# Second norm of a hybrid decoder layer: tile 4 joins the tiles that go through DRAM, rows dealt by stepped reads, two tiles scaled and evicted by ScalarE, the last tile's transposes inside a product

## The chip, the cores and the metric

The kernel runs on one core of a Trainium2 chip. The metric is the device time of one execution in microseconds (us); before the change it is 947.92 us, the median of three runs (947.66 to 949.35).

Names in the profile: PE is TensorE's matmuls, PEld its weight loads, DVE is VectorE, ACT is ScalarE, POOL is GpSimd, SP is SyncE, which issues most of the DMAs. L99 is line 99 of the kernel before. `b<-c,b` says that a buffer of the ring `b` is written from `c` and `b`.

## The reference, cut to what matters

```python
for l in range(DEPTH):                                # DEPTH = 1, 1024 tokens and 16 meta tokens
    u = rmsnorm(h, g_pre_mix[l]); z = u @ w_in[l]     # q, k, v, x_rec, y_rec
    ...                                               # attention and gated recurrence
    mix = jnp.concatenate([attn, rec], axis=-1) @ w_out[l]
    h = h + rmsnorm(mix, g_post_mix[l])
    u = rmsnorm(h, g_pre_ffn[l])                      # the second norm
    f = jnp.square(jax.nn.relu(u @ w_ff1[l])) @ w_ff2[l]
    h = h + rmsnorm(f, g_post_ffn[l])
```

Width is 1024, the feed-forward width 4096, all in float32. Each float32 product is made of three fp32r matmuls (high x high, high x low, low x high: lines 125, 130, 131), so every operand is split into a high part (a cast on ACT, L96) and a low part (a difference on DVE, L99).

## The kernel before, in words

The 1024 tokens are eight tiles of 128 rows. For each tile `out_mm` multiplies the mixed heads by `w_out` into two PSUM banks. `out_norm` takes the sum of squares (ACT, L1052), a power on POOL (L176), scales and adds the residual on DVE (L1058, L1061), stores `h` (SP, L1062) and takes the squares of `h` for the second norm (ACT, L1064, and POOL again). `out_scale` multiplies `h` by the second norm's factor.

What follows needs the second norm's result `u` transposed: features on partitions, tokens along the free axis. There are two ways to it.

- Tiles 0 to 3 (`u2_store`, L1010 to L1018): one DVE operation multiplies `h` by the factor and by `g_pre_ffn` and deals the 1024 columns into four groups, column by column. A DVE transpose of 32x32 blocks follows, a store to DRAM (`u2_dram`) by SP, and four reads back (`u2_read`, L1022), which wait for the store. The result lies in `u2f[0]`, four buffers [128, 16, 2, 32]: 16 groups of 32 tokens, two feature blocks each.
- Tiles 4 to 7 (`out_scale` L1071 and `u2_tiles`, L1083 to L1094): DVE scales, PE transposes eight blocks of 128x128 against the identity into two banks of the tag `o`, and the banks are evicted with `g_pre_ffn` as a column factor: the first four blocks by ACT in four operations of 128 columns (L1094), the last four by DVE in two of 256 (L1088); for tile 6 ACT takes all eight. The result lies in `u2f[1]`, four buffers [128, 2, 512].

The first feed-forward product is one step of a Strassen-like scheme on halves of features and tokens. `u2f[0]` holds the first four tiles and `u2f[1]` the last four, with two buffers for each half of the features. `t_sums` (L1236) makes differences and sums of the four quarters in pieces of tokens, as tiles come in: `t3 = u2f[1][2+i] - u2f[1][i]`, `t2 = t3 + u2f[0][i]`, and the split `ot2` of `t2`. `p1(p)` is the product with the first quarter, `p2(p)` that with the second, evicted by a DVE addition (L1234). `prep_a(p)` loads two blocks of `w_ff1`, makes their sums and differences on DVE (L1109) and splits them (L96, L99). The main loop over 16 blocks then multiplies `ot2` and `ot3` (the split of `t3`).

The order on each engine comes from a scheduler that goes by the order of the code and by a timeline of its own; `behind(name, ins)` pins one instruction behind another on the same engine. Buffers come from rings (`raw` 2, `ws` 5, `a` 16, `b` 17, `c` 8, `d` 4, `e` 2), so a buffer's reuse is a wait too.

Of the kernel before, what the change touches and what calls it, by code (L numbers as in the profile page):

```python
# [9 lines left out]
F32 = mybir.dt.float32  # L10
F32R = mybir.dt.float32r
AF = mybir.ActivationFunctionType
# [25 lines left out]
def hybrid_layer(  # L38
# [961 lines left out]

    u2f = [[slot("c", [P, 16, 2, 32]) for _ in range(4)], [None] * 4]
    u2_dram = dpool.tile([4, 4, P, 2 * P], F32, name="u2_dram")
    gpre_b = slot("ws", [P, D])
    nc.scalar.dma_start(gpre_b, g_pre_ffn[0].partition_broadcast(P))

    def dealt(t_):
        return t_.rearrange("p (k d b) -> p k d b", k=KC, b=4)

    def u2_store(t, h, rs, tmp):
        ins = nc.vector.scalar_tensor_tensor(  # L1010
            tmp.rearrange("p (b k d) -> p k d b", b=4, k=KC), dealt(h), rs,
            dealt(gpre_b), op0=ALU.mult, op1=ALU.mult,
        ).ins
        if t < 3:
            behind(summed[t + 1], ins)
        y = slot("e", [P, D])
        nc.vector.transpose(y, tmp)
        nc.sync.dma_start(u2_dram[t].rearrange("a (d b) r -> (a d) (b r)", b=4), y)  # L1018

    def u2_read(t):  # L1020
        for q in range(4):
            nc.sync.dma_start(  # L1022
                u2f[0][q][:, 4 * t : 4 * t + 4].rearrange("p a k t -> p a (k t)"),
                u2_dram[t, :, :, 64 * q : 64 * q + 64].rearrange("a p r -> p a r"),
            )
# [19 lines left out]
    def out_norm(t, po):  # L1045
# [17 lines left out]
        ssq2 = small.tile([P, 1], F32, name="ssq", tag="ssq")  # L1063
        nc.scalar.activation(xr, h, AF.Square, scale=RMS_SC, accum_out=ssq2)  # L1064
        return h, xr, rstd_of([ssq2])

    def out_scale(t, h, xr, rs2):
        if t < 4:
            u2_store(t, h, rs2, xr)
            return None  # L1070
        nc.vector.tensor_scalar(xr, h, rs2, None, op0=ALU.mult)  # L1071
        return xr

    def u2_tiles(t, xn):
        half = t // 4
        if u2f[half][0] is None:
            u2f[half] = [slot("c", [P, 2, 512]) for _ in range(4)]
        o = (t % 4) * P
        for k4 in range(0, KC, 4):
            pt = bank("o", (P, 4, P))  # L1080
            for i in range(4):
                kc = k4 + i
                nc.tensor.transpose(pt[:, i, :], xn[:, kc * P : (kc + 1) * P], ident)  # L1083
            for i in range(0, 4, 2):
                kc = k4 + i
                dst = u2f[half][kc // 2]
                if k4 and t != 6:
                    nc.vector.tensor_tensor(  # L1088
                        dst[:, :, o : o + P], pt[:, i : i + 2, :],
                        g_ffn_col[:, kc : kc + 2].to_broadcast([P, 2, P]), op=ALU.mult,  # L1090
                    )
                    continue
                for n in range(2):
                    nc.scalar.activation(  # L1094
                        dst[:, n, o : o + P], pt[:, i + n, :], AF.Copy,
                        scale=g_ffn_col[:, kc + n : kc + n + 1],
                    )

    w1v = w_ff1.rearrange("(b k p) c -> b p k c", b=2, p=P)

    def w1_load(dst, b, p, a0, a1):
        c0 = 256 * p
        nc.sync.dma_start(dst, w1v[b][:, :, c0 + P * a0 : c0 + P * a1])

    def combine(dst, x0, x1, op):
        return nc.vector.tensor_tensor(dst, x0, x1, op=op).ins  # L1109

    def rows(t_, c=slice(0, 512)):
        if len(t_.shape) == 4:
            return t_[:, c.start // 32 : c.stop // 32]
        return t_[:, :, c].rearrange("p k (g t) -> p g k t", t=32)

    def operand(tiles):
        pairs = []
        for t_ in tiles:
            hi, lo = pair("b", [P, 2, 512])
            if len(t_.shape) == 4:  # L1120
                split(rows(hi), rows(lo), t_)
            else:
                split(hi, lo, t_)
            pairs.append((hi, lo))
        return pairs

    def product(acc, w, op, first, after=None):
        wh, wl = w
        for kc in range(4):
            hh, ll = op[kc // 2]  # L1130
            mm3(
                acc, (wh[:, kc, :], wl[:, kc, :]), (hh[:, kc % 2, :], ll[:, kc % 2, :]),
                first and kc == 0, kc == 3, after if kc == 0 else None,
            )
# [5 lines left out]
    def prep_a(p, late=None):  # L1140
        r0 = slot("raw", [P, 4, 256])
        w1_load(r0, 0, p, 0, 2)
        r1 = slot("a" if 2 <= p < 14 else "d", [P, 4, 256])
# [22 lines left out]
    def early(b, p0, hl, tag="raw"):  # L1166
        raw = slot(tag, [P, 2, 4, P])
        for k in range(2):
            w1_load(raw[:, k], b, p0 + k, 0, 1)
        split(*hl, raw)  # L1170
        return {p0 + k: (hl[0][:, k], hl[1][:, k]) for k in range(2)}

    a11_early, a12_early = {}, {}

# [61 lines left out]
    def t_sums(c):  # L1236
        for i in range(2):
            combine(t3[i][:, :, c], u2f[1][2 + i][:, :, c], u2f[1][i][:, :, c], ALU.subtract)
            combine(rows(t2[i], c), rows(t3[i], c), rows(u2f[0][i], c), ALU.add)
            hi, lo = ot2[i]  # L1240
            split(hi[:, :, c], lo[:, :, c], t2[i][:, :, c])

    for t in range(8):
        po = pos[t] if t < 4 else out_banks(t)
        out_mm(t, po, range(6 if t < 4 else 0, KC))
        if t > 5:
            u2_tiles(t - 2, xns[t - 2])
        if t == 7:
            t3 = [slot("a", [P, 2, 512]) for _ in range(2)]
            t2 = [slot("a", [P, 2, 512]) for _ in range(2)]  # L1250
# [4 lines left out]
        if 1 <= t <= 4:  # L1255
            u2_read(t - 1)
        if t == 7:
            t_sums(slice(0, 2 * P))
            u2_tiles(6, xns[6])
# [24 lines left out]
    for i in range(2):  # L1284
        behind(urgent, split(*ot3[i], t3[i]))
    token_low = mark[0]
# [3 lines left out]
    def t_rest(k):  # L1290
        i = k % 2
        if k < 2:
            behind(mark[0], combine(rows(u2f[1][i]), rows(u2f[1][i]), u2f[0][i], ALU.subtract))
        elif k < 4:
            behind(mark[0], combine(rows(t2[i]), u2f[0][2 + i], rows(t2[i]), ALU.subtract))
        else:
            hl = pair("a", [P, 2, 512])
            late = mark[0]
            behind(late, split(*hl, t2[i]))
            for n in range(2):  # L1300
                nc.gpsimd.dma_start(t4_dram[:, n, 2 * i : 2 * i + 2, :], f32(hl[n]))
# [339 lines left out]
```

## Time and profile before

| what | before |
|---|---|
| median of three runs | 947.92 us (947.66 to 949.35) |
| the profiled execution | 947.43 us, of it 945.7 in the span of the profile |
| granted TensorE clock | 0.998 |
| PE, weight loads, DVE, ACT, POOL busy | 99%, 83%, 70%, 53%, 14% of the span |
| DVE busy from 290 to 340 us of the span | 42.34 of 50 us |
| chain that ended last | 97% PE |

The profile is one execution. A row of the timeline gives start, duration, engine, line and shapes, and in brackets the engine's idle time before it and what ended that. A group row gives the count, the sum and the mean of the durations, and the idle time before them. Matmuls are pipelined: one lasts 0.39 us, but the next starts 0.23 us after it, so distances are taken from start to start.

### The profile page before, as it was taken

The numbers are of one execution on the slowest core, as the hardware profiler recorded it, in microseconds if no ns is written. First come the engines' busy times: TensorE is split into PE (matmuls) and PEld (weight loads), VectorE is DVE, ScalarE is ACT, GpSimd is POOL, SyncE is SP. The second block draws the span as 40 slices with busy tenths as digits, with TensorE's granted clock in tenths as the row PEclk, the third lists the DMA queues.
The fourth block names the chain that finished last, engine by engine and source line by source line (L and its number), as shares of the span: only waits on it lengthen the run. The fifth ranks groups of instructions, "written<-read, shape, count | busy, mean of one in ns | idle before, by whom it ended". The sixth has DMA issues, their size and how long they took to land.

```text
span 945.7 us, 12177 instructions
## 1 busy us (share of the span) xinstructions
PE 936.2 (99%) x4584; PEld 783.5 (83%) x4584; DVE 664.2 (70%) x848; ACT 504.2 (53%) x845; POOL 133.6 (14%) x205
## 2 busy tenths in 40 slices
PE   9999999999999999999999999999999999999996
PEld 8999999877888878888888888888888888888885
DVE  6667788889877986765544465477667676779883
ACT  8546765679435664443655575654533443445441
POOL 4104436430021100110000000001121000001201
PEclk9999999999999999999999999999999999999999
DMA  8220011104358658574422364335777756547934
GB/s 274 57 67 24 24 46 45 45 23 138 104 182 268 203 189 283 185 251 134 157 89 89 113 216 120 108 112 121 191 169 173 213 179 192 188 132 211 236 65 89
DMA packets 97366, 134.91 MB, mean 143 GB/s; under 512 B 22230, under 2 KB 61158, under 8 KB 97308
## 3 DMA queue, kind: packets, MB, share of 16 engines
q1 hardware_dynamic: 87996, 108.64, 36.1%
q0 software_dynamic: 8880, 24.19, 12.2%
q10 hardware_dynamic: 432, 1.31, 0.4%
q8 instruction: 36, 0.59, 0.3%
q14 instruction: 22, 0.18, 0.1%
HBM read 112.55 MB, written 20.97 MB: 141 GB/s over the span
## 4 chain that ended last, share of the span: by engine, by line
PE 97%; DVE 1%; DMA 1%; ACT 0%; issue 0%; SPq 0%; DVEq 0%
PE ps_acc L131 11%; PE ps_acc L125 11%; PE ps_acc L130 11%; PE ps_pt L130 7%; PE ps_pt L125 6%; PE ps_s L131 6%; PE ps_s L125 6%; PE ps_pt L131 6%; PE ps_s L130 6%; PE ps_o L125 5%; PE ps_o L130 5%; PE ps_o L131 5%; PE ps_o L699 2%; PE ps_acc L924 1%; PE ps_acc L282 1%; PE ps_s L629 1%
## 5 line engine op out<-in xcount | busy, mean ns | idle before, releaser
L99 DVE TENSOR_TENSOR ws<-raw,ws 128x1024 fp32r<-128x1024 f32 (+1 forms) x69 | 83.1, 1204 | 70.9 <-PE ps_o L130 23.0
L96 ACT CAST ws<-raw 128x1024 fp32r<-128x1024 f32 (+1 forms) x68 | 69.8, 1027 | 81.5 <-PE ps_o L130 33.1
L96 ACT CAST ws<-e 128x1024 fp32r<-128x1024 f32 x41 | 43.0, 1049 | 85.1 <-PE ps_o L130 37.8
L99 DVE TENSOR_TENSOR b<-b,b 128x1024 fp32r<-128x1024 f32 (+1 forms) x49 | 57.5, 1176 | 27.6 <-PE ps_o L130 22.3
L125 PE MATMUL ps_acc<-a,ws 128*128 128x512 f32 (+3 forms) x224 | 76.3, 340 | 0.0
L130 PE MATMUL ps_acc<-a,ws 128*128 128x512 f32 (+3 forms) x224 | 76.3, 340 | 0.0
L131 PE MATMUL ps_acc<-a,ws 128*128 128x512 f32 (+3 forms) x224 | 75.7, 338 | 0.0
L99 DVE TENSOR_TENSOR ws<-e,ws 128x1024 fp32r<-128x1024 f32 x41 | 50.1, 1223 | 31.4 <-ACT ws L96 17.9
L96 ACT CAST b<-b 128x1024 fp32r<-128x1024 f32 (+1 forms) x49 | 49.5, 1011 | 41.5 <-DVE b L1109 35.3
L686 POOL TENSOR_SCALAR_AFFINE_SELECT c<-c 128x512 fp32r<-128x512 f32 x64 | 53.2, 846 | 73.6 <-ACT c L96 64.6
L131 PE MATMUL ps_acc<-ws,b 128*128 128x512 f32 (+1 forms) x120 | 46.1, 384 | 0.0
L130 PE MATMUL ps_acc<-ws,b 128*128 128x512 f32 (+1 forms) x120 | 46.1, 384 | 0.0
L125 PE MATMUL ps_acc<-ws,b 128*128 128x512 f32 (+1 forms) x120 | 46.0, 385 | 0.0
L125 PEld LDWEIGHTS ps_acc<-a,ws 128*128 128x128 f32 x224 | 42.2, 188 | 3.1 <-DVE b L933 0.3
L131 PEld LDWEIGHTS ps_acc<-a,ws 128*128 128x128 f32 x224 | 42.1, 188 | 3.0
L130 PEld LDWEIGHTS ps_acc<-a,ws 128*128 128x128 f32 x224 | 42.1, 188 | 2.8
L125 PE MATMUL ps_pt<-ws,b 128*128 128x512 f32 x112 | 44.3, 395 | 0.0
L130 PE MATMUL ps_pt<-ws,b 128*128 128x512 f32 x112 | 44.2, 395 | 0.0
L131 PE MATMUL ps_pt<-ws,b 128*128 128x512 f32 x112 | 44.0, 393 | 0.0
L125 PE MATMUL ps_s<-ws,b 128*128 128x512 f32 x110 | 43.4, 395 | 0.0
L130 PE MATMUL ps_s<-ws,b 128*128 128x512 f32 x110 | 43.3, 393 | 0.0
L131 PE MATMUL ps_s<-ws,b 128*128 128x512 f32 x110 | 43.2, 393 | 0.0
(421 smaller groups left out, 2680.8 us busy)
## 6 DMA issues: line engine op xcount, KB each, us to landing
raw<-in_w_ff_dram SPq DMA_DIRECT2D x59, 512.0 KB, 4.1
e<-in_w_ff_dram SPq DMA_DIRECT2D x43, 512.0 KB, 3.5
a<-in_w_ff_dram SPq DMA_DIRECT2D x12, 512.0 KB, 6.1
s_dram<-a POOLq DMA_DIRECT2D x12, 512.0 KB, 3.8
raw<-in_w_in_dram SPq DMA_DIRECT2D x9, 512.0 KB, 4.0
c<-in_x_dram SPq DMA_DIRECT2D x8, 512.0 KB, 5.1
d<-in_x_dram SPq DMA_DIRECT2D x8, 512.0 KB, 3.3
out_dram<-raw SPq DMA_DIRECT2D x8, 512.0 KB
```

The lines of the kernel that those rows point to most:

```text
L96: cast[0] = nc.scalar.copy(hi, src).ins.name
L99: low = nc.vector.tensor_tensor(lo, src, f32(hi), op=ALU.subtract).ins
L125: ins = nc.tensor.matmul(dst, lh, rh, start=start, stop=False, skip_group_check=True).ins
L130: nc.tensor.matmul(dst, lh, rl, start=False, stop=False, skip_group_check=True)
L131: last_mm[0] = nc.tensor.matmul(dst, ll, rh, start=False, stop=stop, skip_group_check=True).ins.name
L282: last_mm[0] = nc.tensor.matmul(acc[:, :n], w[k // 2][:, kc, :], u[kc][k % 2][:, t0 : t0 + n], start=k == 0 and kc == 0, stop=k == last an ...
L629: nc.tensor.matmul(dst, q[h][:, c], hi, start=True, stop=False, skip_group_check=True,)
L686: nc.gpsimd.affine_select(out=p_[:, :, s], in_=f32(p_[:, :, 0]), pattern=[[0, 4], [g, P]], compare_op=op, fill=0.0, base=0, channel_multip ...
L699: nc.tensor.matmul(two[:, :, oc : oc + w], v, p_.rearrange("p (j i) s c -> p j (i s c)", j=2)[:, :, pc : pc + w], start=n == 0 and k == 0, ...
L924: ins = nc.tensor.matmul(y2_bank[half], (wh, wh, wl)[k][:, kc, :], (uh, ul, uh)[k][:, t0 : t0 + n], start=m % 24 == 0, stop=m % 24 == 23, ...
```

## The change

Five edits:

1. `MOVED = 5`: tile 4 takes the way of tiles 0 to 3 (dealing, 32x32 transpose, store, four reads) and no longer that over PE. So `u2f[1]` gets the same layout [128, 16, 2, 32], and its buffers are taken from the ring at the start.
2. `dealt`: the dealing operation reads `h` and `g_pre_ffn` with a step of four columns and writes each group plainly; before, it read plainly and wrote with a step of 256.
3. Tiles 5 and 6 are scaled by ACT (a Copy with a factor) and not by DVE; ACT evicts all eight blocks of tile 5 too. Only tile 7 keeps DVE's scaling and its two DVE evictions.
4. With the layout, `t_sums`, `t_rest` and the differences run over plain memory, and the splits rearrange on the way (`rows`).
5. The product `p2(1)` is cut in two: its first six matmuls stay, the transposes of tile 7 come next, and the rest is pinned behind them. The weight loads of `prep_a` are pinned behind those of `early` on SP.

```diff
+    MOVED = 5
+    u2f = [[slot("c", [P, 16, 2, 32]) for _ in range(4)] for _ in range(2)]
+    u2_dram = dpool.tile([MOVED, 4, P, 2 * P], F32, name="u2_dram")
...
     def dealt(t_):
-        return t_.rearrange("p (k d b) -> p k d b", k=KC, b=4)
+        return t_.rearrange("p (n b) -> p b n", b=4)
...
-            tmp.rearrange("p (b k d) -> p k d b", b=4, k=KC), dealt(h), rs,
+            tmp.rearrange("p (b n) -> p b n", b=4), dealt(h), rs,
             dealt(gpre_b), op0=ALU.mult, op1=ALU.mult,
...
     def out_scale(t, h, xr, rs2):
-        if t < 4:
+        if t < MOVED:
             u2_store(t, h, rs2, xr)
             return None
-        nc.vector.tensor_scalar(xr, h, rs2, None, op0=ALU.mult)
+        if t == 7:
+            nc.vector.tensor_scalar(xr, h, rs2, None, op0=ALU.mult)
+        else:
+            nc.scalar.activation(xr, h, AF.Copy, scale=rs2)
         return xr
...
-                if k4 and t != 6:
+                dst = by_k(u2f[1][kc // 2][:, o : o + 4])
+                if k4 and t == 7:
...
-            combine(t3[i][:, :, c], u2f[1][2 + i][:, :, c], u2f[1][i][:, :, c], ALU.subtract)
-            combine(rows(t2[i], c), rows(t3[i], c), rows(u2f[0][i], c), ALU.add)
+            combine(t3[i][:, c], u2f[1][2 + i][:, c], u2f[1][i][:, c], ALU.subtract)
+            combine(t2[i][:, c], t3[i][:, c], u2f[0][i][:, c], ALU.add)
             hi, lo = ot2[i]
-            split(hi[:, :, c], lo[:, :, c], t2[i][:, :, c])
+            split(rows(hi, c), rows(lo, c), t2[i][:, c])
...
-    for p in range(2):
-        p2(p, a12_early[p])
-    t_sums(slice(2 * P, 3 * P))
+    p2(0, a12_early[0])
+    y2 = bank("pt")
+    product(y2, a12_early[1], b21, True, kcs=range(2))
+    t_sums(slice(8, 12))
     wa[0] = prep_a(0)
     u2_tiles(7, xns[7])
-    t_sums(slice(3 * P, 4 * P))
+    product(y2, a12_early[1], b21, True, turned[0], kcs=range(2, 4))
+    nc.vector.tensor_tensor(block("11", 1), y2, block("11", 1), op=ALU.add)
+    t_sums(slice(12, 16))
```

Three places show what this does to the order of the instructions.

DVE, from tile 4's residual addition to the first splits of the feed-forward operand, before:

```order
357 L1061 TENSOR_TENSOR raw_3165<-raw_3165,d_3163 128x1024
358 L1017 STREAM_TRANSPOSE e_3106<-d_3080 128x1024
359 L1071 TENSOR_SCALAR d_3163<-raw_3165,rs 128x1024
360 L99 TENSOR_TENSOR a_3190<-raw_3191,a_3189 128x1024
361 L172 SCALAR_TENSOR_TENSOR ms<-sq_3249,sq_3250 128x1
362 L1058 SCALAR_TENSOR_TENSOR raw_3248<-ps_acc_3196,rs,e_2790 128x512
363 L1058 SCALAR_TENSOR_TENSOR raw_3248<-ps_acc_3197,rs,e_2790 128x512
364 L1061 TENSOR_TENSOR raw_3248<-raw_3248,d_3246 128x1024
365 L1088 TENSOR_TENSOR c_3335<-ps_o_3346,gcol 128x2x128
366 L1088 TENSOR_TENSOR c_3336<-ps_o_3346,gcol 128x2x128
367 L1071 TENSOR_SCALAR d_3246<-raw_3248,rs 128x1024
368 L99 TENSOR_TENSOR ws_3277<-raw_3278,ws_3276 128x1024
```

And now, in the line numbers of the changed kernel (L1011 is the dealing operation, L1018 the 32x32 transpose, L1061 and L1064 were L1058 and L1061):

```order
357 L1064 TENSOR_TENSOR raw_3169<-raw_3169,d_3167 128x1024
358 L1018 STREAM_TRANSPOSE e_3110<-d_3084 128x1024
359 L1011 SCALAR_TENSOR_TENSOR d_3167<-raw_3169,rs,ws_2802 128x1024
360 L99 TENSOR_TENSOR a_3197<-raw_3198,a_3196 128x1024
361 L172 SCALAR_TENSOR_TENSOR ms<-sq_3256,sq_3257 128x1
362 L1061 SCALAR_TENSOR_TENSOR raw_3255<-ps_acc_3203,rs,e_2790 128x512
363 L1061 SCALAR_TENSOR_TENSOR raw_3255<-ps_acc_3204,rs,e_2790 128x512
364 L1064 TENSOR_TENSOR raw_3255<-raw_3255,d_3253 128x1024
365 L1018 STREAM_TRANSPOSE e_3189<-d_3167 128x1024
366 L99 TENSOR_TENSOR ws_3288<-raw_3289,ws_3287 128x1024
```

The dealing operation stands where tile 4's scaling stood, its transpose comes behind tile 5's residual addition, and tile 4's two evictions and tile 5's scaling are gone from DVE.

PE around the last tile's transposes (L1083; `ps_s` is the fourth p1, `ps_pt_3562` the second p2, `ps_pt_3653` the third), before:

```order
1820 L131 MATMUL ps_pt_3562<-b_3379,ws_3277 128x512
1821 L130 MATMUL ps_s_3639<-b_3269,b_3383 128x512
1822 L131 MATMUL ps_s_3639<-b_3268,e_3384 128x512
1823 L125 MATMUL ps_s_3639<-b_3272,b_3383 128x512
1824 L130 MATMUL ps_s_3639<-b_3273,b_3383 128x512
1825 L131 MATMUL ps_s_3639<-b_3272,e_3384 128x512
1826 L1083 MATMUL ps_o_3600<-ident,d_3464 128x128 x4
1827 L1083 MATMUL ps_o_3609<-ident,d_3464 128x128 x4
1828 L125 MATMUL ps_s_3639<-b_3272,b_3383 128x512
1829 L130 MATMUL ps_s_3639<-b_3273,b_3383 128x512
1830 L131 MATMUL ps_s_3639<-b_3272,e_3384 128x512
1831 L125 MATMUL ps_pt_3653<-b_3375,a_3512 128x512
```

And now (L1093 are the transposes, `ps_pt_3555` the second p2, `ps_pt_3646` the third):

```order
1818 L125 MATMUL ps_s_3632<-b_3283,b_3374 128x512
1819 L130 MATMUL ps_s_3632<-b_3284,b_3374 128x512
1820 L131 MATMUL ps_s_3632<-b_3283,e_3375 128x512
1821 L1093 MATMUL ps_o_3586<-ident,d_3457 128x128 x4
1822 L1093 MATMUL ps_o_3595<-ident,d_3457 128x128 x4
1823 L125 MATMUL ps_pt_3555<-b_3370,ws_3287 128x512
1824 L130 MATMUL ps_pt_3555<-b_3371,ws_3287 128x512
1825 L131 MATMUL ps_pt_3555<-b_3370,ws_3288 128x512
1826 L125 MATMUL ps_pt_3555<-b_3370,ws_3287 128x512
1827 L130 MATMUL ps_pt_3555<-b_3371,ws_3287 128x512
1828 L131 MATMUL ps_pt_3555<-b_3370,ws_3288 128x512
1829 L125 MATMUL ps_pt_3646<-b_3366,a_3505 128x512
```

Six matmuls of the second p2 now stand behind the transposes, where three of the fourth p1 stood. Between the start of tile 6's product and tile 7's transposes there are 116 matmuls of 512 columns, and 119 before; between these transposes and the first product with `ot2` there are 18, and 15 before.

DVE behind those transposes (L1088 evicts tile 7, L1109 are the sums, L1234 the addition of the third p2), before:

```order
407 L1088 TENSOR_TENSOR c_3335<-ps_o_3609,gcol 128x2x128
408 L1088 TENSOR_TENSOR c_3336<-ps_o_3609,gcol 128x2x128
409 L1109 TENSOR_TENSOR a_3456<-c_3335,c_3333 128x2x128
410 L1109 TENSOR_TENSOR a_3457<-c_3336,c_3334 128x2x128
411 L1109 TENSOR_TENSOR a_3458<-a_3456,c_2793 128x4x2x32
412 L1109 TENSOR_TENSOR a_3459<-a_3457,c_2794 128x4x2x32
413 L99 TENSOR_TENSOR b_3461<-a_3458,b_3460 128x2x128
414 L1234 TENSOR_TENSOR b_3637<-ps_pt_3653,b_3637 128x512
415 L99 TENSOR_TENSOR b_3463<-a_3459,b_3462 128x2x128
416 L99 TENSOR_TENSOR b_3668<-a_3456,b_3667 128x1024
```

And now (L1101, L1124 and L1244 were L1088, L1109 and L1234; L1290 is the addition of the second p2; the split at 401 is of tile 6's sums):

```order
400 L1101 TENSOR_TENSOR c_2799<-ps_o_3595,gcol 128x2x4x32
401 L99 TENSOR_TENSOR b_3456<-a_3452,b_3455 128x4x2x32
402 L1101 TENSOR_TENSOR c_2800<-ps_o_3595,gcol 128x2x4x32
403 L1124 TENSOR_TENSOR a_3449<-c_2799,c_2797 128x256
404 L1290 TENSOR_TENSOR d_3525<-ps_pt_3555,d_3525 128x512
405 L1124 TENSOR_TENSOR a_3450<-c_2800,c_2798 128x256
406 L1124 TENSOR_TENSOR a_3451<-a_3449,c_2793 128x256
407 L1124 TENSOR_TENSOR a_3452<-a_3450,c_2794 128x256
408 L99 TENSOR_TENSOR b_3454<-a_3451,b_3453 128x4x2x32
409 L99 TENSOR_TENSOR b_3456<-a_3452,b_3455 128x4x2x32
410 L1244 TENSOR_TENSOR b_3630<-ps_pt_3646,b_3630 128x512
411 L99 TENSOR_TENSOR b_3661<-a_3449,b_3660 128x16x2x32
```

The addition of the second p2 has come into the row, and both splits of 256 elements (of the last quarter of the tokens) stand ahead of the addition of the third p2; before, one of them stood behind it.

More of the change, by code (lines that the diff above doesn't have):

```diff
@@ L1119, in operand, with product @@
             hi, lo = pair("b", [P, 2, 512])
[L1120 to L1123, printed above, removed]
+            split(rows(hi), rows(lo), t_)
             pairs.append((hi, lo))
         return pairs
-    def product(acc, w, op, first, after=None):
+    def product(acc, w, op, first, after=None, kcs=range(4)):
         wh, wl = w
-        for kc in range(4):
+        for kc in kcs:
             hh, ll = op[kc // 2]
@@ L1132, in product @@
                 acc, (wh[:, kc, :], wl[:, kc, :]), (hh[:, kc % 2, :], ll[:, kc % 2, :]),
-                first and kc == 0, kc == 3, after if kc == 0 else None,
+                first and kc == 0, kc == 3, after if kc == kcs[0] else None,
             )
@@ L1141, in prep_a @@
         r0 = slot("raw", [P, 4, 256])
-        w1_load(r0, 0, p, 0, 2)
+        behind(loads[0], w1_load(r0, 0, p, 0, 2))
         r1 = slot("a" if 2 <= p < 14 else "d", [P, 4, 256])
@@ L1284, in hybrid_layer @@
     for i in range(2):
-        behind(urgent, split(*ot3[i], t3[i]))
+        behind(urgent, split(*map(rows, ot3[i]), t3[i]))
     token_low = mark[0]
@@ L1298, in t_rest @@
             late = mark[0]
-            behind(late, split(*hl, t2[i]))
+            behind(late, split(*map(rows, hl), t2[i]))
             for n in range(2):
```

65 lines of the change are left out of this document (36 added, 29 removed).

## The prediction

> **What bounds the kernel now.** I read the page first, its busy shares and the engines of the chain that ended last, and then the waits of TensorE and the stages around the change.
>
> ```profile
> span 945.7 us, 12177 instructions
> PE 936.2 (99%) x4584; PEld 783.5 (83%) x4584; DVE 664.2 (70%) x848; ACT 504.2 (53%) x845; POOL 133.6 (14%) x205
> ...
> PE 97%; DVE 1%; DMA 1%; ACT 0%; issue 0%; SPq 0%; DVEq 0%
> ```
>
> TensorE (PE) is busy in all but 9.5 us of the span, and 97% of the chain is its own work. So an edit can gain only by taking PE work away or by ending a PE wait. The waits of PE show two, both in the first microseconds:
>
> ```profile
> PE ps_acc L309 <- DVE base_e L563: 1.5, 1, 1.5
> PE ps_o L358 <- DVE d L248: 0.6, 1, 0.6
> ```
>
> The change lies between 262 us (first second-norm) and 350 us (second feed-forward block). The stages there, with columns PE, weight loads, DVE, ACT and POOL busy, clock, DMA share and GB/s:
>
> ```profile
> 262.00:290.00 28.00, 28.00 (x123) 22.69 (x122) 22.82 (x24) 9.10 (x22) 6.77 (x12) 1.00 0.66 213
> 290.00:340.00 50.00, 50.00 (x235) 41.07 (x234) 42.34 (x65) 31.57 (x65) 6.72 (x12) 1.00 0.73 228
> 340.00:350.00 10.00, 9.93 (x44) 7.64 (x43) 6.82 (x12) 5.94 (x9) 1.08 (x2) 1.00 0.49 151
> ```
>
> PE is full until 340 at a granted clock of 1.00. VectorE (DVE) is busy 42.34 of 50 us from 290 to 340, so it is the engine that could make PE late. Only the last stage has a gap, 0.07 us by busy time. Busy time hides the rest, because pipelined matmuls overlap, so I go by starts:
>
> ```profile
> 343.81 0.46 PE L125 MATMUL ps_s<-b,e 128*128 128x512 f32 x1
> 344.10 0.39 PE L130 MATMUL ps_s<-b,e 128*128 128x512 f32 x1
> 344.57 0.50 PE L131 MATMUL ps_acc<-b,e 128*128 128x512 f32 x1
> 344.90 0.39 PE L125 MATMUL ps_acc<-b,e 128*128 128x512 f32 x1
> ```
>
> **Term 1, eight transposes fewer.** Tile 4 no longer passes PE. What its eight transposes cost now:
>
> ```profile
> 300.75 0.40 PE L131 MATMUL ps_s<-a,b 128*128 128x512 f32 x1
> 300.98 1.03 PE L1083 MATMUL ps_o<-ident,d 128*128 128x128 f32 x8
> 301.77 0.48 PE L125 MATMUL ps_pt<-ws,b 128*128 128x512 f32 x1
> ```
>
> A matmul of 512 columns starts 0.23 us after the one before (300.75 to 300.98). The group holds PE from 300.98 to 301.77, **0.79 us**. This gain is certain as long as nothing makes PE wait for longer than now.
>
> **Term 2, the wait at 344.** Four starts from 343.81 to 344.90 are 1.09 us apart, where three steps of 0.23 make 0.69: 0.40 us are lost. The matmul at 344.57 waits for the low half of a weight split on DVE. That comes out of a run of DVE work without a gap, which begins where DVE itself waits for PE (the third product p2, `ps_pt`):
>
> ```profile
> 331.78 0.74 DVE L1088 TENSOR_TENSOR c<-ps_o,gcol 128x256 f32<-128x256 f32 x2
> 334.29 0.42 DVE L99 TENSOR_TENSOR b<-a,b 128x256 fp32r<-128x256 f32 x1 [0.42 <-ACT b L96]
> 335.20 0.69 DVE L1234 TENSOR_TENSOR b<-ps_pt,b 128x512 f32<-128x512 f32 x1 [0.49 <-PE ps_pt L131]
> 335.81 1.55 DVE L99 TENSOR_TENSOR b<-a,b 128x256 fp32r<-128x256 f32 x2
> 343.83 0.68 DVE L99 TENSOR_TENSOR e<-raw,e 128x512 fp32r<-128x512 f32 x1
> ```
>
> After the change PE reaches both ends of this run 0.79 us earlier, so by itself the wait would stay. But the new order puts both small splits of the sums ahead of that addition; now one of them stands behind it, in the pair at 335.81. It is a split of 256 elements, about 0.4 us (0.42 at 334.29). So the weight split ends 0.79 + 0.4 earlier, at 344.51 - 1.19 = 343.32, and PE without the wait wants it at 344.10 + 0.23 - 0.07 - 0.79 = 343.47 (0.07 is what the step 343.81 to 344.10 is over 0.23). The wait goes, with 0.15 us to spare: **0.40 us**. Its bounds are 0 and 0.40.
>
> This needs the splits to be through before the addition's new time, 335.20 - 0.79 = 334.41. The last tile's transposes start now at
>
> ```profile
> 330.65 1.04 PE L1083 MATMUL ps_o<-ident,d 128*128 128x128 f32 x8
> ```
>
> and stand behind three matmuls fewer in the new order: 330.65 - 0.79 - 0.69 = 329.17. DVE evicts 1.13 us after that start (331.78), so from 330.30. Between there and the addition stand ten DVE instructions: nine of 256 elements, of about 0.33 us from start to start (pairs of 0.74), and the moved addition of 512, 0.61 (335.20 to 335.81): 3.6 us, to 333.9. Half a microsecond is left, if ScalarE's casts in between are no later than now. The moved addition waits for the six matmuls behind the transposes (329.17 + 0.79 + 6 x 0.23 + 0.4 = 331.7), which is when DVE comes to it; three sums and two splits queue behind it, and PE's next product waits for these.
>
> **What DVE and ACT get and lose.** Durations in the groups of the stage:
>
> ```profile
> L1061 DVE TENSOR_TENSOR raw<-raw,d 128x1024 f32<-128x1024 f32 x8 | 9.8, 1224 | 0.2
> L1010 DVE SCALAR_TENSOR_TENSOR d<-raw,rs,ws 128x1024 f32<-128x1024 f32 x4 | 8.3, 2087 | 0.0
> L1017 DVE STREAM_TRANSPOSE e<-d 128x1024 f32<-128x1024 f32 x4 | 5.0, 1244 | 0.1
> L99 DVE TENSOR_TENSOR b<-c,b 128x1024 fp32r<-128x1024 f32 x4 | 4.8, 1220 | 0.4 <-ACT b L96 0.4
> L1071 DVE TENSOR_SCALAR d<-raw,rs 128x1024 f32<-128x1024 f32 x4 | 3.0, 754 | 2.3 <-POOL rs L176 2.3
> L99 DVE TENSOR_TENSOR b<-a,b 128x1024 fp32r<-128x1024 f32 x2 | 2.4, 1219 | 0.0
> L1088 DVE TENSOR_TENSOR c<-ps_o,gcol 128x256 f32<-128x256 f32 x6 | 2.3, 417 | 1.7 <-PE ps_o L1083 1.7
> ```
>
> DVE gains one dealing operation and one 32x32 transpose (tile 4), and loses three scalings (tiles 4, 5, 6) and four evictions (tiles 4 and 5): 2.09 + 1.24 - 3 x 0.75 - 4 x 0.42 = **-0.6 us**, if the dealing keeps its 2.09. Splits that write or read runs of 32 cost what plain ones cost (1220 against 1219), so the new layout of the fifth to eighth tiles is priced at nothing, and the sums keep their sizes.
>
> The dealing operation is the unknown. It writes with a step now (2087 ns against 1224 for a plain operation with two inputs) and will read both inputs with a step of four elements and write plainly. No row shows a stepped read of this length. Below stands 1.22, and 4.17 above, twice the stepped row, if the two stepped inputs pay one after the other. I take 2.09, the same operation with the step on its other side; at 1.22 DVE gets 5 x 0.87 us more room and PE gains nothing further.
>
> The Trainium skill (SBUF — State Buffer, Specifications) gives 16-byte lines that need two hits each for full bandwidth. A step of four float32 is one hit a line, so by that rule the stepped reads stay dear; the stepped write's 2087 ns agree, and no row here shows the read. By the rule at the price of the write the sum is the same; paid per input it is rival C.
>
> ACT gains two scalings of 1024 and no evictions on balance (four fewer for tile 4, four more for tile 5):
>
> ```profile
> 301.73 1.13 ACT L1094 ACTIVATE c<-ps_o,gcol 128x128 f32<-128x128 f32 x4
> 302.83 1.06 ACT L96 CAST ws<-raw 128x1024 fp32r<-128x1024 f32 x1
> 302.21 0.56 POOL L176 TENSOR_TENSOR rs<-ms,half_pow 128x1 f32<-128x1 f32 x1
> ```
>
> Tile 5's scaling stands where tile 4's evictions stood and waits for POOL's power, which ends at 302.77. A cast of 1024 took 1.06, so it ends near 303.9, and the casts behind it come 1.0 us later than now. Their operands' product starts at 313.76 - 0.79; the cover is several microseconds, and DVE's low halves, queued behind them, have the same. Tile 6's scaling (ACT near 318) is read by PE's transposes near 323. ACT is busy 31.57 of 50 us; without cover each scaling would cost 1.06.
>
> **Tile 4's way through DRAM** adds a store and four reads to SP's queue:
>
> ```profile
> 294.27 0.51 SPq L1018 DMA_DIRECT2D u_dram<-e  x1
> 298.30 3.84 SPq L1022 DMA_DIRECT2D c<-u_dram  x4
> 302.24 0.53 SPq L1062 DMA_DIRECT2D out_dram<-raw  x1
> c<-u_dram SPq DMA_DIRECT2D x16, 128.0 KB, 3.9
> ```
>
> The store stands behind the output at 302.24, so at 302.8; the reads follow 4.03 later as tile 3's did, take 3.84 to issue and 3.9 to land: 314.5. The first sum that reads them waits for tile 5's evictions anyway (transposes from 312.2, then 2 x 1.13 of ACT: 315.2). SP's next entry, tile 6's output, was issued at 312.75, after these reads' issue (310.6), so the weight loads behind it keep their times. Queued behind that sum on DVE are tile 7's norm and scaling, which end 2.9 us before PE needs them. So a delay costs nothing up to about 0.7 + 2.9 = 3.6 us.
>
> **The sum.** -0.79 - 0.40 = -1.19 us. The profiled execution took 947.43 (945.7 in the span, 1.7 around it) and comes to 946.24; it lies 0.49 under the median of the runs, 947.92. So I predict 947.92 - 1.19 = **946.7 us**, 0.13% less. No later stage has a wait on PE that could go or PE work that goes.
>
> **The rivals.**
>
> A, the forecast: both terms hold, 946.7; with term 2 kept at nothing 947.1. Chance 0.70.
>
> B, a new wait takes the gain. The margins at the last tile are 0.15 and 0.5 us. If the tile's sums are one cast later (0.4 to 1.06 us), PE waits once at the second operand's product and once at the weight split: 0.3 to 1.9 us, thus 947.0 to 948.6. Speaks for it: DVE without a gap from 335.81. Against: DVE has 0.6 us less to do. Chance 0.12, nearly all within 0.2%.
>
> C, the stepped reads cost 4.17 each. DVE then has 5 x 2.08 - 0.6 = 9.8 us more in 262 to 340, where it idles 5.18 + 7.66 = 12.8 us. Half of that idle time sits in front of POOL's powers and PE's results and can't be filled, I estimate, so 3.4 us reach PE, and all 9.8 if none can: 947.92 - 1.19 + 3.4 to 9.8 = 950.1 to 956.5, slower. It decides from the point where 3.1 us reach PE: 2.8 us an operation with no idle time filled, 4.1 with half. For it: two stepped inputs instead of one stepped output. Against: plain operations read two inputs at 1.22, so the two reads run side by side. Chance 0.11.
>
> D, tile 4's trip is late. At twice tile 3's time (another 4.03 + 3.9) it is 7.9 late, 4.3 over the cover: 947.92 - 1.19 + 4.3 = 951.0. DMA share was 0.73 in that stage, so the first trips ran under load already. Chance 0.03.
>
> E, over 0.2% faster: nothing in PE's 9.5 idle us, most of it at the two ends, would give 1.9 us. Only runs that spread would; the three went from 947.66 to 949.35. Chance 0.04.
>
> **How the numbers follow.** 0.2% is 1.9 us, about what a measurement of this kernel can tell from no change. Within it fall A and B, 0.82; slower are C and D, 0.14; faster E, 0.04. The range reaches from 945.8, about a microsecond under the forecast for the spread of the runs, up to 949.8, which takes in B and the start of C; about 0.15 is left out, most of it C's dear end.
>
> **What would show it.** Term 1: 24 transposes instead of 32, and matmuls 0.23 apart where tile 4's stood. Term 2: no step over 0.3 us between matmul starts near 343. Dealing: the mean of the operation at 1.2, 2.1 or 4.2 us. ACT: scalings of about 1.06 us and PE transposes of tile 6 without a wait. DRAM: the first sum's idle time ended by ACT and not by a DMA. A PE wait for DVE between 312 and 345 would make the forecast wrong, and its releaser tells B, C and D apart.

## The result, and the profile after

The changed kernel takes **946.68 us** (median of 22 runs, 946.0 to 948.73); the kernel before 947.95 us (22 runs, 947.29 to 949.54). The ratio is 0.9988, with a 95% interval of 0.9983 to 0.9994: 0.12% less, 1.1 us; the two medians lie 1.27 us apart. The prediction was 946.7, with a range from 945.8 to 949.8.

The page of the changed kernel, its span and its busy shares:

```profile
span 945.6 us, 12176 instructions
PE 936.1 (99%) x4576; PEld 783.4 (83%) x4576; DVE 663.6 (70%) x843; ACT 506.4 (54%) x847; POOL 134.1 (14%) x205
```

TensorE (PE) has eight instructions fewer, VectorE (DVE) 0.6 us less to do and ScalarE (ACT) 2.2 us more. Yet the spans of the two profiled executions are as good as equal (945.7 and 945.6). The reason lies ahead of the change: this execution came to the changed stage later. The rows are a matmul of the mixing product that both kernels have, and one of the main loop, first of the kernel before:

```profile
260.92 0.39 PE L130 MATMUL ps_o<-a,b 128*128 128x512 f32 x1
...
407.58 0.39 PE L125 MATMUL ps_s<-b,ws 128*128 128x512 f32 x1
```

and the same two of the changed kernel:

```profile
262.09 0.39 PE L130 MATMUL ps_o<-a,b 128*128 128x512 f32 x1
...
407.57 0.39 PE L125 MATMUL ps_s<-b,ws 128*128 128x512 f32 x1
```

Between them lie 146.66 us before and 145.48 now: **1.18 us less**, where the sum said 1.19. The 1.17 us by which the stage began later arose between 20 and 28 us, among instructions that the change doesn't touch. From the second of these matmuls to the last, every run here takes 530.6 us. So the distance of these two matmuls, called **the stage** from here on, leaves out most of what whole runs spread over (2.7 us here). Each stage is that of one execution, and none was taken twice. Of the kernels below that should have an equal one, e2 and e6 lie 0.03 and 0.05 us from the changed kernel and e4 lies 0.04 from the kernel before, so differences under 0.1 us are not read.

The stages after, with the columns of before (PE, weight loads, DVE, ACT and POOL busy, clock, DMA share, GB/s):

```profile
290.00:340.00 50.00, 50.00 (x231) 40.88 (x230) 42.95 (x61) 33.58 (x67) 6.46 (x13) 1.00 0.83 253
340.00:350.00 10.00, 10.00 (x45) 8.02 (x44) 6.94 (x12) 6.04 (x9) 1.08 (x2) 1.00 0.48 150
```

The gap of PE in the last row is gone. Where tile 4's transposes stood, between p1 and the next product, matmuls now follow each other:

```profile
301.92 0.39 PE L131 MATMUL ps_s<-a,b 128*128 128x512 f32 x1
302.15 0.39 PE L125 MATMUL ps_pt<-ws,b 128*128 128x512 f32 x1
```

They start 0.23 us apart. And where the wait was, at the matmul that reads the weights' low half:

```profile
344.17 0.39 PE L125 MATMUL ps_s<-b,e 128*128 128x512 f32 x1
344.40 0.39 PE L130 MATMUL ps_s<-b,e 128*128 128x512 f32 x1
344.63 0.45 PE L131 MATMUL ps_acc<-b,e 128*128 128x512 f32 x1
344.92 0.39 PE L125 MATMUL ps_acc<-b,e 128*128 128x512 f32 x1
```

The steps are 0.23, 0.23 and 0.29: 0.06 us remain of 0.40. The DVE rows behind it, splits, addition and weight split:

```profile
334.60 0.76 DVE L99 TENSOR_TENSOR b<-a,b 128x256 fp32r<-128x256 f32 x2
335.55 0.69 DVE L1244 TENSOR_TENSOR b<-ps_pt,b 128x512 f32<-128x512 f32 x1 [0.20 <-PE ps_pt L131]
...
343.84 0.68 DVE L99 TENSOR_TENSOR e<-raw,e 128x512 fp32r<-128x512 f32 x1
```

Both small splits stand ahead of the addition, which waits 0.20 us for PE. That is all that was left of the half microsecond.

### The profile page after: what moved, and what is told of

It reads as the page before. It is cut to its first block, busy times and chain, and to the rows that moved or that the text cites. A ratio compares the mean times of both kernels' runs of the same rounds, so it can differ in the third digit from the quotient of the medians.

```text
span 945.6 us, 12176 instructions
## 1 busy us (share of the span) xinstructions
PE 936.1 (99%) x4576; PEld 783.4 (83%) x4576; DVE 663.6 (70%) x843; ACT 506.4 (54%) x847; POOL 134.1 (14%) x205
## 4 chain that ended last, share of the span: by engine, by line
PE 98%; DVE 1%; issue 0%; ACT 0%; DVEq 0%
PE ps_acc L125 11%; PE ps_acc L131 11%; PE ps_acc L130 11%; PE ps_pt L130 7%; PE ps_pt L125 7%; PE ps_pt L131 7%; PE ps_s L125 6%; PE ps_s L131 6%; PE ps_s L130 6%; PE ps_o L125 5%; PE ps_o L130 5%; PE ps_o L131 5%; PE ps_o L699 2%; PE ps_acc L924 1%; PE ps_s L629 1%; PE ps_s L633 1%
```

## The experiments

The theory: the 1.18 us are PE's eight transposes (0.79) and the wait at 344 (0.40), and DVE, ACT and the DMAs only keep pace. The rivals: the cut of p2(1) or the dealing brought it; or eight transposes are cheaper than they look, and the gain comes from somewhere else. Times are medians; ratios are against executions of the kernel before made with each run (medians of 947.63 to 947.95), with 95% intervals. Taken against these, the medians differ from the kernel before as the stages do, within 0.5 us, but for e11 (0.7) and e12 (1.0).

| run | us | ratio | stage, us | stage against after |
|---|---|---|---|---|
| before | 947.95 | | 146.66 | +1.18 |
| after | 946.68 | 0.9988 [0.9983, 0.9994] | 145.48 | |
| e1 four moved | 949.75 | 1.0020 [1.0012, 1.0029] | 148.73 | +3.25 |
| e2 step on the write | 946.71 | 0.9986 [0.9978, 0.9995] | 145.52 | +0.03 |
| e3 p2(1) whole | 946.68 | 0.9990 [0.9981, 0.9998] | 145.90 | +0.41 |
| e4 cut alone | 947.91 | 1.0001 [0.9992, 1.0010] | 146.70 | +1.22 |
| e5 six moved | 955.29 | 1.0081 [1.0067, 1.0095] | 154.41 | +8.93 |
| e6 plain dealing | 946.59 | 0.9987 [0.9978, 0.9996] | 145.53 | +0.05 |
| e7 double dealing | 958.32 | 1.0114 [1.0098, 1.0129] | 156.76 | +11.28 |
| e8 DVE scales | 947.03 | 0.9990 [0.9981, 0.9998] | 146.11 | +0.63 |
| e9 transposes twice | 947.22 | 0.9998 [0.9989, 1.0007] | 146.66 | +1.17 |
| e10 four moved, DVE | 948.93 | 1.0012 [1.0004, 1.0021] | 147.73 | +2.25 |
| e11 six moved, GpSimd | 967.10 | 1.0198 [1.0184, 1.0212] | 166.86 | +21.38 |
| e12 late sums | 952.98 | 1.0056 [1.0043, 1.0070] | 152.98 | +7.50 |

### The price of eight transposes (e9)

```diff
-            for i in range(4):
+            for i in [0, 1, 2, 3] * (2 if t == 5 else 1):
                 kc = k4 + i
```

> The changed kernel with tile 5's eight transposes made twice into the same banks, all else as it was. It prices eight transposes at the place beside the removed ones. Theory (term 1: they cost the distance of their starts, PE has no slack to hide them): the stage from the mixing product to the main loop is 0.8 us longer than in the changed kernel (145.5 to 146.3), and the time lies at 947.2 to 947.7. Rival (PE would have waited there anyway, so that the time came from somewhere else): the stage stays within 0.2 us of 145.5.

PE around tile 5's transposes, in this run:

```profile
311.99 1.91 PE L1093 MATMUL ps_o<-ident,d 128*128 128x128 f32 x16
313.65 0.48 PE L125 MATMUL ps_acc<-b,a 128*128 128x512 f32 x1
```

Sixteen hold PE for 1.66 us; in the changed kernel the eight go from 313.26 to 314.05, 0.79. The eight more cost 0.87. The stage grew by 1.17, where 0.8 was expected; the other 0.3 are PE steps longer than in the changed kernel, among them those at 344 (0.30 and 0.33 instead of 0.23 and 0.29). So PE hides nothing of a transpose, and the wait at 344 comes back in part in a run whose order on DVE differs a little.

### The cut of p2(1), undone and alone (e3, e4)

e3 undoes the cut and keeps all else:

```diff
-    p2(0, a12_early[0])
-    y2 = bank("pt")
-    product(y2, a12_early[1], b21, True, kcs=range(2))
+    for p in range(2):
+        p2(p, a12_early[p])
...
-    product(y2, a12_early[1], b21, True, turned[0], kcs=range(2, 4))
-    nc.vector.tensor_tensor(block("11", 1), y2, block("11", 1), op=ALU.add)
```

> The changed kernel with the second product p2 in one piece again and the last tile's transposes behind it. One small split then stands behind the third p2's addition again. My theory (term 2): the wait of TensorE for the weight split near 343 comes back with 0.3 to 0.4 us between three starts, and the time is 0.3 to 0.4 over the changed kernel, 947.0 to 947.1. Rival (the wait went because VectorE has less to do): no wait, 946.7.

PE at the old wait, in e3:

```profile
343.36 0.39 PE L130 MATMUL ps_s<-b,e 128*128 128x512 f32 x1
343.75 0.50 PE L131 MATMUL ps_acc<-b,e 128*128 128x512 f32 x1
344.08 0.40 PE L125 MATMUL ps_acc<-b,e 128*128 128x512 f32 x1
```

The wait is back: 0.39 and 0.33 instead of 0.23 and 0.29. On DVE one small split stands behind the addition again, as before the change. The stage is 0.41 longer: 0.20 of it are these two steps, 0.11 a step of 0.34 at the product of the sums (334.44), and the rest lies in smaller amounts elsewhere. The median of the whole runs can't show it.

e4 is the kernel before with the same cut and nothing else (the diff of e3 turned round).

> The kernel before with the cut of the second product p2 alone. The order built from it still leaves one small split behind the third p2's addition on VectorE. My theory: 32 transposes and the wait near 344 both stay, so the time is that of before, 947.9 within 0.2. Rival (moving the transposes ahead by itself ends the wait): 0.4 under before, 947.5, and no step over 0.3 us between starts near 344.

PE at the same place in e4:

```profile
344.05 0.40 PE L130 MATMUL ps_s<-b,e 128*128 128x512 f32 x1
344.52 0.50 PE L131 MATMUL ps_acc<-b,e 128*128 128x512 f32 x1
```

The wait stands as before (0.47 instead of 0.23), and the stage has its old length. On DVE one small split stands behind the addition here too. So the cut alone brings nothing, and the changed kernel without it loses 0.41: term 2 needs both.

### Four tiles moved (e1, e10)

e1 has `MOVED = 4`: tile 4 goes over PE as before, but ACT scales it and evicts all its blocks.

> The changed kernel with tile 4 back on TensorE (four tiles through DRAM), all else as changed; ScalarE scales and evicts tile 4 too. My theory: 32 transposes again, so TensorE has 0.79 us more work; VectorE loses 3.3 us of dealing and transposing, ScalarE gets 1.06 of scaling and 8 evictions (2.2 us). Time 0.8 us over the changed kernel if ScalarE hides its 3.3 us, up to 2 us over it if it does not, thus 947.5 to 948.7. Rival (the gain came only from the new order at the last tile): the same time as the changed kernel, 946.7.

This missed, by far to the dear side. PE's two longest waits behind 290 us in e1 (total, times, longest):

```profile
PE ps_s L131 <- DVE e L99: 0.6, 1, 0.6
PE ps_acc L125 <- ACT b L96: 0.4, 1, 0.4
```

Besides the transposes' 0.79, PE's steps from start to start are too long at 335 (by 1.2 us in sum), at 345 (0.2) and at 356 (0.9). Two causes were open: what ACT now does of tile 4 (its scaling, and four evictions that DVE made in the kernel before), or the order, in which the third p2's addition stands ahead of both small splits. e10 takes the first away:

```diff
-        if t == 7:
+        if t in (4, 7):
             nc.vector.tensor_scalar(xr, h, rs2, None, op0=ALU.mult)
...
-                if k4 and t == 7:
+                if k4 and t in (4, 7):
```

> The changed kernel with four moved tiles, as in the earlier run with four, but tile 4 is scaled by VectorE and its last four blocks evicted by VectorE, as in the kernel before; only tiles 5 and 6 load ScalarE. Theory (in the earlier run ScalarE, with one scaling and four evictions more, made its casts of the sums late): the waits at the second operand's product go, and the stage is 0.8 to 1.3 us longer than the changed kernel's 145.5, thus 146.3 to 146.8, time 947.3 to 948.2. Rival (it was the order, with the addition of the third p2 ahead of both small splits, whoever scales): the stage stays near the 148.7 of the earlier run, time 949.5 to 950.2.

It came out between the two. PE at the second operand's product in e10:

```profile
335.98 0.40 PE L131 MATMUL ps_pt<-b,a 128*128 128x512 f32 x1
336.73 0.50 PE L125 MATMUL ps_acc<-b,e 128*128 128x512 f32 x1 [0.36 <-ACT b L96]
```

With that load taken from ACT, and the order that the scheduler made of it, 1.0 of the 3.25 us is gone. The long steps at the sums' product fell only from 1.2 to 0.9 us, with one small split still behind the addition, and 0.4 us are lost at a new place (384.65, where PE waits for the split of a later weight block). How much of that is the order and how much DVE's own load wasn't separated. What both runs show: the other edits without the move are slower than the kernel before. DVE's total is not the reason, for the move makes it larger: DVE is busy 663.6 us in the changed kernel and 661.6 in e10, ACT 506.4 and 507.4. Why DVE comes in time at the last tile with five moved tiles and late with four stays open.

### The dealing (e2, e6, e7)

e2 puts the step back on the write, as in the kernel before:

```diff
-        return t_.rearrange("p (n b) -> p b n", b=4)
+        return t_.rearrange("p (n b) -> p n b", b=4)
...
-            tmp.rearrange("p (b n) -> p b n", b=4), dealt(h), rs,
+            tmp.rearrange("p (b n) -> p n b", b=4), dealt(h), rs,
```

> The changed kernel with the dealing of before: plain reads, writes with a step. My theory: the step costs the same on either side, so the dealing operation takes 2.09 us instead of the 2.07 of the changed kernel, and the time stays within 0.1 us of 946.7. Rival (the stepped reads bring part of the gain): 0.2 us or more over the changed kernel, and a wait of TensorE near 343.

e6 deals without any step (`"p (b n) -> p b n"` in `dealt`).

> The changed kernel with the dealing operation reading and writing plainly, so that columns are not dealt and the result is not the reference's; only its duration is wanted. My theory: the operation falls from 2.07 to 1.22 us, VectorE is 4.3 us lighter, and the time stays at 946.7 within 0.2, since TensorE no longer waits for VectorE there. Rival (a wait on the dealing is still in the time): 0.3 us or more under the changed kernel.

The dealing operation's group in the changed kernel, mean in ns behind the comma:

```profile
L1011 DVE SCALAR_TENSOR_TENSOR d<-raw,rs,ws 128x1024 f32<-128x1024 f32 x5 | 10.3, 2066 | 1.1 <-POOL rs L176 1.1
```

and in e6:

```profile
L1011 DVE SCALAR_TENSOR_TENSOR d<-raw,rs,ws 128x1024 f32<-128x1024 f32 x5 | 6.4, 1273 | 0.8 <-POOL rs L176 0.8
```

Stepped writes took 2093 in e2. Step on reads, on the write, or none: the stage stays within 0.05 us. PE gains nothing from DVE's 4 us of savings in e6. e7 goes the other way and makes each dealing operation twice (`for _ in range(2):` around it), which is rival C made real.

> The changed kernel with every dealing operation made twice, one after the other, so that it takes 4.14 us: rival C of the prediction as a fact, 10.3 us more on VectorE. My theory prices it at 3.4 us of waiting (half of VectorE's idle time usable) to 9.8 (none): 950.1 to 956.5, most likely 953. If VectorE's idle time took it all: 946.7.

PE's four longest waits behind 290 us in e7:

```profile
PE ps_acc L125 <- ACT b L96: 3.7, 1, 3.7
PE ps_s L125 <- ACT b L96: 1.6, 1, 1.6
PE ps_acc L130 <- DVE b L99: 1.5, 1, 1.5
PE ps_s L131 <- DVE e L99: 1.0, 1, 1.0
```

DVE got 10.3 us more (ten operations of 2.06 instead of five), and the stage 11.28: more than all of it. The mechanism was C's. Its ceiling of 9.8 was too low, because behind the longest wait seven steps between matmuls are 0.43 us instead of 0.23, as in the next runs too; that is 1.4 us, and without it the stage would be 9.9 us longer.

### ACT's scalings (e8)

`if t > 4` instead of `if t == 7`: DVE scales tiles 5, 6 and 7.

> The changed kernel with tiles 5 and 6 scaled by VectorE again (0.75 us each) instead of ScalarE. In the order built from it one small split stands behind the third p2's addition again. My theory: the wait near 343 comes back in part, 0.2 to 0.4 us over the changed kernel, 946.9 to 947.1, through the order and not through the 1.5 us of work. Rival (ScalarE's scalings cost as much as they free): the same time or less, 946.7 or under.

PE at the second operand's product in e8:

```profile
334.74 0.40 PE L131 MATMUL ps_pt<-b,a 128*128 128x512 f32 x1
335.12 0.50 PE L125 MATMUL ps_acc<-b,e 128*128 128x512 f32 x1
335.58 0.53 PE L130 MATMUL ps_acc<-b,e 128*128 128x512 f32 x1
```

PE steps 0.38 and 0.46, where the changed kernel has 0.23. The stage pays 0.63, where 0.2 to 0.4 was expected, and about 0.5 of it here and not near 343. The expectation put it down to the order alone. But DVE's first small split, which stands ahead of the addition in both kernels, comes 0.88 us later in the stage too (335.10 - 261.71 against 334.60 - 262.09), so that order alone did not make the splits late. What the two scalings of 0.75 do by themselves wasn't separated. So 0.63 of the 1.18 us hang on ACT's scaling of these two tiles. The shares don't add up: this 0.63, e3's 0.41 and the transposes' 0.87 are more than 1.18.

### Six tiles moved (e5, e11), and late sums (e12)

e5 has `MOVED = 6`, by the same reckoning another 0.79 us for PE.

> The changed kernel with tile 5 through DRAM as well (six tiles). TensorE loses another eight transposes, 0.79 us; VectorE gets another dealing of 2.07 and a transpose of 1.24, 3.3 us, and loses nothing; ScalarE loses 1.06 of scaling and 2.2 of evictions. My theory (VectorE's margin at the last tile is under half a microsecond): the added 3.3 us push VectorE's sums of the last tile past TensorE, which waits 1 to 3.3 us there, so 946.7 - 0.8 + 1 to 3.3 = 946.9 to 949.2. Rival (VectorE's idle time of 7 us between 290 and 340 takes it): 945.9.

It cost 8.9 us instead. PE at the second operand's product, and the stages around it (columns as above), in e5:

```profile
338.90 0.50 PE L125 MATMUL ps_acc<-b,e 128*128 128x512 f32 x1 [3.19 <-ACT b L96]
340.34 0.79 PE L130 MATMUL ps_acc<-b,e 128*128 128x512 f32 x1 [0.94 <-DVE b L99]
340.93 0.63 PE L131 MATMUL ps_acc<-b,e 128*128 128x512 f32 x1
341.36 0.63 PE L125 MATMUL ps_acc<-b,e 128*128 128x512 f32 x1
```

```profile
335.00:340.00 5.00, 1.22 (x5) 0.42 (x3) 5.00 (x12) 3.44 (x6) 0.35 (x1) 0.94 0.00 0
339.50:346.20 6.70, 5.86 (x14) 4.59 (x15) 5.95 (x10) 3.30 (x5) 0.65 (x1) 0.50 0.52 157
```

DVE is full while PE waits, and then the clock stands at 0.50: twelve steps between matmuls are 0.43 instead of 0.23, which alone is 2.4 us. Ahead of it, SP's queue holds tile 5's store and reads where weight loads stood:

```profile
317.22 2.56 SPq L1023 DMA_DIRECT2D c<-u_dram  x4
323.46 0.35 SPq L1065 DMA_DIRECT2D out_dram<-raw  x1
323.86 1.33 SPq L1121 DMA_DIRECT2D a<-in_w_ff_dram  x2
325.28 1.78 SPq L1121 DMA_DIRECT2D raw<-in_w_ff_dram  x2
```

In the changed kernel the two loads into `a` go out at 316.02, and the next one into `raw` ahead of tile 7's output too:

```profile
319.90 0.37 SPq L1121 DMA_DIRECT2D raw<-in_w_ff_dram  x1
```

In e5 they stand behind that output, and DVE's first sum of weights waits for a load:

```profile
331.24 0.69 DVE L1124 TENSOR_TENSOR d<-raw,d 128x512 f32<-128x512 f32 x1 [0.85 <-DMA raw<-in_w_ff_dram]
```

In the changed kernel this sum is made at 324.68. So in e5 the sums and splits of the weights fall among those of the last tile, up to 339.95, ahead of its small splits. This speaks for the queue, but the trace doesn't tell what share of the 8.9 us is the queue's.

e11 tested that queue by giving tile 5's store and reads to GpSimd:

```diff
...
-            nc.sync.dma_start(
+            (nc.gpsimd if t == 5 else nc.sync).dma_start(
                 u2f[t // 4][q][:, 4 * (t % 4) : 4 * (t % 4) + 4].rearrange(
```

> The changed kernel with six moved tiles, as in the earlier run with six, but tile 5's store and its four reads are issued by GpSimd's queue and not by SyncE's. Theory (in the earlier run these entries stood in SyncE's queue ahead of weight loads, and the loads' delay made the casts and splits late): the PE waits of 0.9, 3.6 and 1.4 us go for the greater part, the stage is 144.7 to 147, and the time 945.9 to 948.2. Rival (tile 5's own way through DRAM is too long for the sums that read it, whichever queue issues it): a wait of over 2 us stays at the product that reads the sums, released by VectorE or ScalarE whose own idle time a read of tile 5 ended; stage above 149, time above 950.

Far worse, and by something that neither theory had. GpSimd's and ACT's rows in e11:

```profile
320.33 0.80 POOL L1023 DMA_DIRECT2D c<-u_dram  x1 [5.08 <-DMA u_dram<-e]
...
330.33 1.10 POOL L176 TENSOR_TENSOR rs<-ms,half_pow 128x1 f32<-128x1 f32 x2
```

```profile
330.94 1.15 ACT L1081 ACTIVATE d<-raw,rs 128x1024 f32<-128x1024 f32 x1 [7.71 <-POOL rs L176]
```

The reads wait for the store and are issued 3 us apart, and the power for tile 6 (the first of the two in the row at 330.33) stands behind them on GpSimd; ACT's scaling waits 7.7 us for it, and PE's transposes wait for the scaling. So the run doesn't tell e5's causes apart. Whether six tiles would gain with tile 5's DMAs on a queue that holds nobody up stays open.

e12 gives a known delay: the last tile's second sum seven times per half, twelve DVE operations more.

```diff
-            combine(t2[i][:, c], t3[i][:, c], u2f[0][i][:, c], ALU.add)
+            for _ in range(7 if c.start == 12 else 1):
+                combine(t2[i][:, c], t3[i][:, c], u2f[0][i][:, c], ALU.add)
```

> The changed kernel, with the second sum of the last tile's tokens made seven times for each half of the features instead of once: twelve more VectorE operations of 256 elements, about 0.33 us each, ahead of the splits, 4.0 us in all. The output stays the same. It makes PE wait for the splits by a known delay, for two questions. First, the margin: with 0.5 us left the wait is 3.5 us in sum, in one or two steps; without margin 4.0. Second, the clock: if a single wait between the 2.0 us that brought no slow matmuls and the 3.6 us that did is enough, matmuls 0.43 apart follow for some us and the time is 952 to 954; if the waits are too short for it, matmuls stay 0.23 apart and the time is 949.5 to 951.

PE at that product in e12:

```profile
339.45 0.80 PE L125 MATMUL ps_acc<-b,e 128*128 128x512 f32 x1 [4.87 <-ACT b L96]
...
343.49 0.63 PE L125 MATMUL ps_acc<-b,e 128*128 128x512 f32 x1
343.92 0.63 PE L130 MATMUL ps_acc<-b,e 128*128 128x512 f32 x1
```

PE waits 4.87 us, more than the 4.0 added: the scheduler also moved the third p2's addition (0.6 us) ahead of the splits, and DVE came to the sums about a microsecond later. So the run says nothing on the margin, nor on waits between 1.6 and 3.2 us. It shows the slow matmuls once more: nine steps of 0.43, in a stage 7.50 longer and a time (952.98) that was expected for a wait long enough to bring them.

## Why the prediction was right, point by point

**Term 1 (0.79) held, and was a little too small.** Tile 4's group is gone and the matmuls there are 0.23 apart. But 0.79 is the distance to the next matmul's start alone, and that matmul (301.77) was itself followed late:

```profile
302.09 0.40 PE L130 MATMUL ps_pt<-ws,b 128*128 128x512 f32 x1
```

This is 0.32 after it instead of 0.23. So the eight transposes cost 0.88, and e9 prices eight in the same stage at 0.87.

**Term 2 (0.40) held but for 0.06, with less to spare than said.** The rows at 344 keep 0.06 of it, so it was worth 0.34. The last tile's transposes start at 330.29 - 1.17 = 329.12 (329.17 predicted). The three matmuls fewer ahead of them are there, though not as counted ahead (119 and 116 from the start of tile 6's product): the traces have 117 before and 114 now from the start of tile 7's product. I put the end of the weight split at 343.32; it ends at 343.84 + 0.68 - 1.17 = 343.35 on the clock of before (the stage began 1.17 later). The splits I had through at 333.9; they end at 334.60 + 0.76 - 1.17 = 334.19. Half a microsecond of margin was 0.2. The addition came at 335.55 - 1.17 = 334.38, as predicted (334.41). e3 shows that without the cut the wait returns, e4 that the cut alone doesn't end it.

**That the sum met 1.18 to 0.01 is in part luck.** The terms measured 0.88 and 0.34, together 1.22, and 0.04 were lost in small amounts over the other steps: one term was 0.09 too small, the other 0.06 too large. That the median came to 946.68 where 946.7 was said is luck as well, for the interval of the ratio alone is 1.0 us wide.

**The dealing stayed at 2.09: right,** and its place between the bounds was the main risk. Stepped reads took 2.07. The rule of the Trainium skill (SBUF — State Buffer, Specifications), that a 16-byte line needs two hits for full bandwidth, agrees in direction: 2066 ns against 1273 in e6, 1.6 times. Two stepped inputs don't pay one after the other.

**DVE's balance of -0.6 us: right** (664.2 to 663.6 on the pages).

**ACT's scalings: the size was off.** I took a cast's 1.06; they take 1.15:

```profile
L1081 ACT ACTIVATE d<-raw,rs 128x1024 f32<-128x1024 f32 x2 | 2.3, 1152 | 1.0 <-POOL rs L176 1.0
```

The cover held them: no PE wait follows. In e1, where ACT has a third scaling and eight evictions more, waits do.

**Tile 4's trip: hidden, as said.** Its store and reads on SP, and the first sum on DVE:

```profile
303.73 0.38 SPq L1019 DMA_DIRECT2D u_dram<-e  x1
...
308.05 2.52 SPq L1023 DMA_DIRECT2D c<-u_dram  x4
```

```profile
316.18 0.68 DVE L1124 TENSOR_TENSOR a<-c,c 128x512 f32<-128x512 f32 x1
```

Less 1.17 the store is at 302.56 (302.8 predicted) and the sum at 315.01 (315.2). DVE doesn't idle ahead of the sum, for a DMA or for ACT. The weight loads behind tile 6's output did not quite keep their times: the output went out at 315.15 - 1.17 = 313.98 instead of 312.75 and the loads 0.3 to 0.4 us later than before, without a wait of PE.

**The rivals.** B didn't come, but was nearer than its 0.12 said: in e1, e3, e8, e9 and e10, each a small step from this kernel, PE's steps are too long at exactly B's two places. C's mechanism exists (e7) but not its premise; its price of at most 956.5 was too low by 1.8 us, since it had no term for the slow matmuls behind a long wait. D did not happen with one tile more; with a second one (e5) PE waits long, but that tile 5's own trip came too late isn't shown.

**What was not run.** e1 and e10 leave out the move, e2 the stepped reads, e3 the cut and e8 ACT's scalings. The move without the other edits, and the changed kernel without the pinned weight loads of edit 5, have no run.

## What to carry to other kernels

Where PE is busy from end to end, an edit is worth the PE time between starts that it takes away, as long as every feeder keeps its margin. That time is more than the removed group's own: count the step behind it too (0.09 of 0.88 here). So list the margins at the next two or three places where PE reads fresh operands, and see which engine order they hang on. To see a gain of a microsecond among runs that spread over more than two, measure between two instructions that both kernels have, around the change. A second helping of the same edit is priced anew: the fifth tile, with its other edits, gained 1.2 us, the sixth lost 8.9.

## What the runs showed of the hardware that was not expected

A long wait of PE costs more than itself. After idle times of 3.19 (e5), 3.7 (e7), 4.87 (e12), 3.6 and 5.7 us (e11) six to twelve steps between matmuls are 0.43 us instead of 0.23, which adds 1.2 to 2.4 us, and the granted clock reads 0.50 there (in e5 from 339.5 to 346.2 us, in e7 from 344.5 to 347.5). After idle times of up to 1.6 us (e7) the steps are not longer; nothing between 1.6 and 3.19 was measured. The Trainium skill (TensorE: Matmul & The Clock Gate, The HAM clock gate) has it that the clock falls to half after an idle window of about 3.4 us and comes back after about as long a stretch of work. The runs agree in kind. In size they leave two things open: e5's idle time of 3.19 us lies a little under 3.4, though the starts around it are 3.59 apart (335.32 to 338.90), and e5's clock stayed low for 6.7 us.

Also, DMAs issued by GpSimd that wait for a store hold up GpSimd's own arithmetic (e11): four reads are issued 3 us apart, the first when the store has landed, and the step for tile 6's norm, whose input ACT had ready at 318.0, begins behind them at 330.0.
